# Weight words of the paired heads moved from 128 to 64 bytes into their buffers

## The chip, the cores and the metric

The kernel runs on one core of one Trainium2 chip. The metric is the device time of one launch in microseconds (us), the lowest being best. Before the change it took 828.53 us (median of 3 runs, 827.48 to 829.98).

## The reference

One decoder block on x (1 x 512 x 2048, float32). A normed input is multiplied by w_in (2048 x 6808) to give queries, keys, values and gate paths of two head groups. Group A has 8 heads of 128 with compressed, selected and windowed attention; group B has 16 heads of 64 with a window of 128 and a sink. Both are gated, joined, multiplied by w_out (2048 x 2048), added to x and normed again.

```
h = _rmsnorm(x, norm_g[l]);  proj = h @ w_in[l]
(qa, kca, vca, ksa, vsa, kwa, vwa, za, ga, qb, kb, vb, zb) = jnp.split(proj, offsets, axis=-1)
o_a = gates[..., 0:1] * o_cmp + gates[..., 1:2] * o_sel + gates[..., 2:3] * o_win
y_a = o_a.reshape(B, S, WIDTH_A) * jax.nn.silu(za)
o_b = _banded_attention(qb, _rope(kb), vb, WIN_B, sink=sinks);  y_b = o_b * jax.nn.silu(zb)
x = x + jnp.concatenate([y_a, y_b], axis=-1) @ w_out[l];  return _rmsnorm(x, final_g)
```

## The kernel before

All products of float32 data are made of two words per number, a high word (`hi`, rounded by the copy into float32r) and the rest (`lo`). `mm3` (L126) gives one product as three matmuls: high by high, low by high, high by low. ScalarE makes the high word of a unit of 1,024 weights per partition and VectorE the low one (`split`, L642 to L644, for the paired heads; `load_unit`, L89 to L99, elsewhere).

**Where the words lie.** `words(place)` (L86) takes a buffer of 1,088 float32 words per partition, which is 4,352 bytes or 17 times 256, and hands out 1,024 of them that begin `place` words in. There are three such buffers for the high and three for the low words, and they turn over. Three places are in use: MOVING = 0, EVEN = 16 (64 bytes) and STILL = 32 (128 bytes). In the built program every one of the six buffers begins 128 bytes past a multiple of 256. So words at MOVING lie 128 bytes past a multiple of 256, words at EVEN 192 bytes past, and words at STILL 0 bytes past. Every slice of 128 or 256 of them that a matmul takes begins a multiple of 512 bytes further on, so it lies at the same place modulo 256.

**The stages.** (1) To about 206 us: the keys and values of group A, the compressed keys, and head 0. Here either 512 columns of x (`xh`, `xl`) move past weights that stand still, at place EVEN, or the weights move (256 or 408 columns, place MOVING). (2) From 206.85 to 621.23 us: the paired heads, 1 to 14 (`pair`, L689). Here a head's query and gate projection is made by seven half-size products (`prod`, L668) in place of eight: 7 products of 8 steps of 3 matmuls, 168 for a head and 2,352 for the 14, each with 128 weight columns standing still and 256 columns moving. The weights come from `unit` (L658), the only user of STILL. What moves is `xh`, `xl`, `pu` or parts of `VH`, `VL`, `KH`, `KL`; all of these slices begin 192 bytes past a multiple of 256. (3) Head 15 by `plain` (L772), 512 columns moving, place EVEN. (4) From about 685 us: w_out, where the weights move (256 columns, or 512 in its first quarter) and the activations stand still; place MOVING, and EVEN in the first quarter.

In what follows the **step** of a matmul is the place modulo 256 of the weights that are loaded while it runs (those of the next matmul), less the place modulo 256 of its own moving data. It is 64 bytes in stage 2 now (0 less 192, modulo 256), 64 in the attention's own matmuls and in most of stage 4 (192 less 128), and 0 in the 512-column matmuls at place EVEN. Where a paired head's matmul is followed by one of the attention whose still operand (`VH`, `VB` and the like) lies at 192, the step is 0 for one matmul.

**What sets the order.** A scheduler puts the instructions of the attention of the head before between the matmuls of `pair`, from its own model of their times, and `hooks` (L674) do so by hand in heads 8 to 14. So a stretch of the paired heads' matmuls is broken every so often by a few transposes and attention matmuls.

Of the kernel before, what the change touches and what calls it, by code (L numbers as in the profile page):

```python
# [25 lines left out]
SCALE_A = 128 ** -0.5  # L26
SCALE_B = 64 ** -0.5
CMP = 32
MOVING, EVEN, STILL = 0, 16, 32
WARM = 40  # L30
FIRST = 1
TAB_W = 512 + NQ * CMP + 256
# [3 lines left out]
def hybrid_block(ctx, tc, xT, xtm, w0, w1s, w2s, wz, wq, wkb, wo0, wos, cw1, cw2, cpos, rope, tabs, sinks, gT, fg, out):  # L36
# [49 lines left out]
    def words(place):  # L86
        return [wp.tile([P, 1088], F32R, name=nm, tag=nm)[:, place:place + 1024] for nm in ("whi", "wlo")]

    def load_unit(src, width, rawp=None, opening=False, place=EVEN):  # L89
        rw = rawp.tile([P, 1024], F32, name="raw", tag="raw") if rawp else raw()  # L90
        hi, lo = words(place)
        last["dma"] = (nc.scalar if opening else nc.sync).dma_start(rw[:, :width], src).ins
        if opening:
            dve.tensor_copy(hi[:, :width], rw[:, :width])
        else:
            last["hi"] = act.activation(hi[:, :width], rw[:, :width], AF.Copy).ins  # L96
        last["lo"] = dve.tensor_tensor(out=lo[:, :width], in0=rw[:, :width], in1=hi[:, :width].bitcast(F32),  # L97
                                       op=ALU.subtract).ins
        return hi, lo  # L99
# [81 lines left out]
    for k in range(KT):  # L181
        if k == 0:
            hi, lo = load_unit(w0[0, :, 0, 0:512], 512, opening=True)
            xr = load_x(k)
        else:
            xr = load_x(k)
            hi, lo = load_unit(w0[0, :, k // 2, (k % 2) * 512:(k % 2) * 512 + 512], 512)
# [150 lines left out]
    for u in range(KT // 2):  # L338
        hi, lo = load_unit(w0[1, :, u], 1024)
# [302 lines left out]
    def split(hi, lo, src):  # L642
        act.activation(hi, src, AF.Copy)  # L643
        last["lo"] = dve.tensor_tensor(out=lo, in0=src, in1=hi.bitcast(F32), op=ALU.subtract).ins  # L644
# [11 lines left out]
                nc.sync.dma_start(k[1][:, CMP:].bitcast(F32).rearrange("p (m c) -> p m c", c=256), fw[0, e])  # L656

    def unit(raw):  # L658
        hi, lo = words(STILL)
        split(hi, lo, raw)  # L660
        return hi, lo

# [26 lines left out]
    def pair(h, early=(), hooks=None):  # L689
# [26 lines left out]
        if wide:  # L716
            d = wb.tile([P, 256], F32, name="dd", tag="dd")
        x1 = load(c1, 3)
        u0 = unit(x1)
        x2 = load(c2, 0)  # L720
        u3 = unit(x2)
        if wide:
            sm = load(c5, 0, 2)
# [10 lines left out]
        prod(pa[:, H0], u3, "p", True, hooks)  # L734
        plus(d, d, pa[:, H0])
        u2 = unit(x3)
        prod(pb[:, H0], u2, "21", False, hooks)
        act.activation(zr[:, H1], pb[:, H0], AF.Copy)
# [365 lines left out]
    for u in range(8):  # L1104
        hi, lo = load_unit(wo0[:, u], 1024)
# [354 lines left out]
```

## Time and profile before

| | |
|---|---|
| median of 3 runs | 828.53 us (827.48 to 829.98) |
| the profiled execution | 826.69 us, its span from first to last instruction 824.9 us |
| TensorE matmuls | busy 797.2 us, 97% of the span |
| weight loads | busy 750.0 us, 91% |
| VectorE, ScalarE | 83%, 64% |
| mean granted clock of TensorE | 0.999 of full speed |

The span is the core's time from first to last instruction; the rest of the execution's time lies around it. A matmul's row has its start and how long it took. Matmuls overlap, so the time that one costs is the distance from its start to the start of the next, while its own duration also holds its way through the array. Starts are given to 10 ns, so a distance is read over many matmuls, or from durations, which are given in ns.

### The profile page before, as it was taken

The numbers are of one execution on the slowest core, as the hardware profiler recorded it, in microseconds if no ns is written. First come the engines' busy times: TensorE is split into PE (matmuls) and PEld (weight loads), VectorE is DVE, ScalarE is ACT, GpSimd is POOL, SyncE is SP. The second block draws the span as 40 slices with busy tenths as digits, with TensorE's granted clock in tenths as the row PEclk, the third lists the DMA queues.
The fourth block names the chain that finished last, engine by engine and source line by source line (L and its number), as shares of the span: only waits on it lengthen the run. The fifth ranks groups of instructions, "written<-read, shape, count | busy, mean of one in ns | idle before, by whom it ended". The sixth has DMA issues, their size and how long they took to land.

```text
span 824.9 us, 15435 instructions
## 1 busy us (share of the span) xinstructions
PE 797.2 (97%) x5782; PEld 750.0 (91%) x5782; DVE 685.4 (83%) x1271; ACT 529.4 (64%) x1103; POOL 76.4 (9%) x69
## 2 busy tenths in 40 slices
PE   9999999999999999999999989999999999999996
PEld 8788898988999999999999989989888788999996
DVE  7869786865898989998898789989977588977895
ACT  6734456662677867868776568766866776553545
POOL 4500002012011011011010000000000000000000
PEclk9999999999999999999999999999999999999999
DMA  9655886899712314412321685656595336597835
GB/s 320 206 200 166 290 301 195 272 333 353 223 52 66 104 40 141 154 51 79 116 78 63 195 206 135 186 145 166 139 314 183 91 102 218 138 302 181 259 79 204
DMA packets 60954, 145.29 MB, mean 176 GB/s; under 512 B 6352, under 2 KB 19920, under 8 KB 60880
## 3 DMA queue, kind: packets, MB, share of 16 engines
q1 hardware_dynamic: 57424, 132.26, 48.7%
q0 software_dynamic: 3168, 11.54, 8.1%
q8 instruction: 45, 0.74, 0.4%
q10 hardware_dynamic: 288, 0.52, 0.2%
q14 instruction: 29, 0.24, 0.1%
HBM read 121.65 MB, written 20.55 MB: 172 GB/s over the span
## 4 chain that ended last, share of the span: by engine, by line
PE 75%; DVE 9%; ACT 6%; DMA 5%; issue 3%; POOL 1%; SPq 0%; DVEq 0%; ACTq 0%
PE pj L127 13%; PE pj L129 13%; PE pj L128 13%; PE oa L128 4%; PE oa L129 4%; PE oa L127 4%; PE bank L129 4%; PE bank L127 4%; PE bank L128 3%; PE sp L567 3%; DVE wlo L644 2%; DMA raw<-wq 2%; ACT whi L643 1%; DVE raw L703 1%; DMA xr<-xT 1%
## 5 line engine op out<-in xcount | busy, mean ns | idle before, releaser
L127 PE MATMUL pj<-xh,whi 128*128 128x256 f32 (+1 forms) x560 | 170.7, 305 | 8.7 <-DVE sums L907 2.6
L129 PE MATMUL pj<-xh,wlo 128*128 128x256 f32 (+1 forms) x560 | 170.1, 304 | 1.7 <-DVE wlo L644 1.7
L128 PE MATMUL pj<-xl,whi 128*128 128x256 f32 (+1 forms) x560 | 168.8, 301 | 0.0
L643 ACT ACTIVATE whi<-raw 128x1024 fp32r<-128x1024 f32 x98 | 103.0, 1054 | 55.3 <-PE pj L128 33.2
L644 DVE TENSOR_TENSOR wlo<-raw,whi 128x1024 fp32r<-128x1024 f32 x98 | 121.4, 1242 | 12.7 <-ACT whi L643 12.3
L127 PEld LDWEIGHTS pj<-xh,whi 128*128 128x128 f32 x560 | 105.4, 188 | 15.8 <-ACT whi L643 3.0
L129 PEld LDWEIGHTS pj<-xh,wlo 128*128 128x128 f32 x560 | 105.6, 189 | 7.0 <-DVE wlo L644 2.5
L128 PEld LDWEIGHTS pj<-xl,whi 128*128 128x128 f32 x560 | 105.4, 188 | 4.2
L97 DVE TENSOR_TENSOR wlo<-raw,whi 128x512 fp32r<-128x512 f32 (+2 forms) x74 | 81.3, 1104 | 33.5 <-ACT whi L96 33.0
L96 ACT ACTIVATE whi<-raw 128x1024 fp32r<-128x1024 f32 (+1 forms) x73 | 65.5, 901 | 53.1 <-PE pj L128 17.3
L127 PE MATMUL pj<-pu,whi 128*128 128x256 f32 x224 | 64.2, 287 | 2.9 <-DVE sums L908 1.5
L129 PE MATMUL pj<-pu,wlo 128*128 128x256 f32 x224 | 63.2, 282 | 0.5 <-DVE wlo L644 0.5
L128 PE MATMUL pj<-pu,whi 128*128 128x256 f32 x224 | 63.3, 283 | 0.0
L703 DVE TENSOR_TENSOR raw<-raw 128x1024 f32<-128x1024 f32 x46 | 59.1, 1285 | 0.2
L128 PE MATMUL oa<-wlo,xh 128*128 128x256 f32 (+1 forms) x168 | 50.9, 303 | 0.7 <-DVE wlo L1008 0.7
L127 PE MATMUL oa<-whi,xh 128*128 128x256 f32 (+1 forms) x168 | 50.4, 303 | 1.0 <-DVE sums L904 1.0
L129 PE MATMUL oa<-whi,xl 128*128 128x256 f32 (+1 forms) x168 | 50.3, 302 | 0.0
L127 PEld LDWEIGHTS pj<-pu,whi 128*128 128x128 f32 x224 | 42.3, 189 | 4.2 <-issue 1.6
L129 PEld LDWEIGHTS pj<-pu,wlo 128*128 128x128 f32 x224 | 42.3, 189 | 1.0 <-DVE wlo L644 0.9
L128 PEld LDWEIGHTS pj<-pu,whi 128*128 128x128 f32 x224 | 42.2, 188 | 0.0
L536 DVE TENSOR_TENSOR pl<-tp,ph 128x512 fp32r<-128x512 f32 x56 | 37.7, 683 | 4.9 <-ACT ph L535 4.8
L535 ACT ACTIVATE ph<-tp 128x512 fp32r<-128x512 f32 x56 | 32.1, 588 | 12.4 <-PE tp L930 8.4
(372 smaller groups left out, 2325.6 us busy)
## 6 DMA issues: line engine op xcount, KB each, us to landing
raw<-wq SPq DMA_DIRECT2D x65, 512.0 KB, 4.1
raw<-cw SPq DMA_DIRECT2D x16, 512.0 KB, 5.2
raw<-wos SPq DMA_DIRECT2D x15, 512.0 KB, 5.0
raw<-wq POOLq DMA_DIRECT2D x10, 512.0 KB, 5.5
rw<-wos SPq DMA_DIRECT2D x10, 512.0 KB, 5.2
xr<-xT SPq DMA_DIRECT2D x16, 256.0 KB, 5.1
raw<-w SPq DMA_DIRECT2D x8, 512.0 KB, 4.4
fd<-ft SPq DMA_DIRECT2D x4, 1024.0 KB, 6.0
```

Source lines behind the costliest of these rows:

```text
L96: last["hi"] = act.activation(hi[:, :width], rw[:, :width], AF.Copy).ins
L97: last["lo"] = dve.tensor_tensor(out=lo[:, :width], in0=rw[:, :width], in1=hi[:, :width].bitcast(F32), op=ALU.subtract).ins
L127: pe.matmul(ps, ah, bh, start=first, stop=False, skip_group_check=go_on)
L128: pe.matmul(ps, ah, bl, start=False, stop=False, skip_group_check=go_on)
L129: recent["mm"] = pe.matmul(ps, al, bh, start=False, stop=last, skip_group_check=go_on).ins
L535: act.activation(ph, tp, AF.Copy)
L536: dve.tensor_tensor(out=pl, in0=tp, in1=ph.bitcast(F32), op=ALU.subtract)
L567: pe.matmul(sp[:, a:b], qq[:, qs], kk[0][:, ko:ko + b - a], start=pi == 0, stop=pi == 2)
L643: act.activation(hi, src, AF.Copy)
L644: last["lo"] = dve.tensor_tensor(out=lo, in0=src, in1=hi.bitcast(F32), op=ALU.subtract).ins
L703: return dve.tensor_tensor(out=out, in0=a, in1=b, op=op).ins
```

## The change

`unit` takes its words from place EVEN, 64 bytes into the buffer, in place of STILL, 128 bytes in, and the name STILL goes. The weights of the paired heads then begin 192 bytes past a multiple of 256, as the data that move past them do, and the step of their matmuls is 0 in place of 64. Nothing else differs: in the built programs the same instructions stand in the same order on every engine, and the buffers lie where they lay.

```
-MOVING, EVEN, STILL = 0, 16, 32
+MOVING, EVEN = 0, 16
...
     def unit(raw):
-        hi, lo = words(STILL)
+        hi, lo = words(EVEN)
         split(hi, lo, raw)
         return hi, lo
```

## Rows read from the trace of the kernel before

**Rows 1.** The page: engines' busy time, and the granted clock in 40 slices.
```profile
PE 797.2 (97%) x5782; PEld 750.0 (91%) x5782; DVE 685.4 (83%) x1271; ACT 529.4 (64%) x1103; POOL 76.4 (9%) x69
...
PEclk9999999999999999999999999999999999999999
```

**Rows 2.** Chain of waits, 205 to 620 us: share of the stretch by line.
```profile
by line: PE pj L127 17.1%; PE pj L129 16.6%; PE pj L128 16.3%; PE sp L567 5.9%; DVE wlo L644 4.3%; issue 4.1%; DMA raw<-wq 3.1%; ACT whi L643 2.9%; DVE raw L703 2.6%; PE tp L605 2.3%; PE op L611 1.4%; PE op L613 1.4%; PE op L612 1.4%; DVE t
```

**Rows 3.** Waits, 205 to 620 us: us in total, times, longest.
```profile
ACT whi L643 <- PE pj L128: 27.0, 16, 4.2
```

**Rows 4.** Timeline, TensorE, 206 to 621 us: first and last matmul of the paired heads.
```profile
206.85 0.28 PE L127 MATMUL pj<-xh,whi 128*128 128x256 f32 x1
...
621.23 0.28 PE L129 MATMUL pj<-KH,wlo 128*128 128x256 f32 x1
```

**Rows 5.** Timeline near 355 us: a matmul and the weight load beside it, then 357 us.
```profile
355.28 0.28 PE L128 MATMUL pj<-xl,whi 128*128 128x256 f32 x1
355.28 0.19 PEld L129 LDWEIGHTS pj<-xh,wlo 128*128 128x128 f32 x1
...
357.43 0.28 PE L129 MATMUL pj<-xh,wlo 128*128 128x256 f32 x1
```

**Rows 6.** Timeline near 400 us: first and last of ten paired-head matmuls.
```profile
400.11 0.28 PE L129 MATMUL pj<-xh,wlo 128*128 128x256 f32 x1
...
401.17 0.28 PE L129 MATMUL pj<-xh,wlo 128*128 128x256 f32 x1
```

**Rows 7.** Groups by form, 355.29 to 357.4 us: count, busy us, mean ns.
```profile
L128 PE MATMUL pj<-xl,whi 128*128 128x256 f32 x7 | 1.9, 276 | 0.0
```

**Rows 8.** Groups by form, 400.12 to 401.1 us.
```profile
L129 PE MATMUL pj<-xh,wlo 128*128 128x256 f32 x3 | 0.8, 281 | 0.0
```

**Rows 9.** Groups by form, 230.8 to 231.14 us: around one step of 0.
```profile
L611 PE MATMUL op<-ph,VH 128*128 128x256 f32 x1 | 0.3, 288 | 0.0
L128 PE MATMUL pj<-xl,whi 128*128 128x256 f32 x1 | 0.3, 283 | 0.0
...
L127 PE MATMUL pj<-xh,whi 128*128 128x256 f32 x1 | 0.3, 281 | 0.0
```

**Rows 10.** Timeline, 357.5 to 358.1 us: behind a step of 0 at 357.43.
```profile
357.55 0.28 PE L611 MATMUL op<-ph,VH 128*128 128x256 f32 x1
...
358.02 0.28 PE L127 MATMUL pj<-pu,whi 128*128 128x256 f32 x1
```

**Rows 11.** Timeline, 42 to 46 us: 512 columns, step 0, first and last of ten.
```profile
42.83 0.39 PE L127 MATMUL bank<-xh,whi 128*128 128x512 f32 x1
...
44.87 0.39 PE L127 MATMUL bank<-xh,whi 128*128 128x512 f32 x1
```

**Rows 12.** Timeline, 628 to 631 us: 512 columns, step 0, behind attention matmuls.
```profile
628.45 0.40 PE L128 MATMUL pj<-xl,whi 128*128 128x512 f32 x1
628.68 0.40 PE L129 MATMUL pj<-xh,wlo 128*128 128x512 f32 x1
628.91 0.39 PE L127 MATMUL pj<-xh,whi 128*128 128x512 f32 x1
629.14 0.40 PE L128 MATMUL pj<-xl,whi 128*128 128x512 f32 x1
629.38 0.39 PE L129 MATMUL pj<-xh,wlo 128*128 128x512 f32 x1
629.61 0.39 PE L127 MATMUL pj<-xh,whi 128*128 128x512 f32 x1
...
630.51 0.39 PE L128 MATMUL pj<-xl,whi 128*128 128x512 f32 x1
```

**Rows 13.** Groups by form: the units' words on VectorE and ScalarE.
```profile
L644 DVE TENSOR_TENSOR wlo<-raw,whi 128x1024 fp32r<-128x1024 f32 x98 | 121.4, 1242 | 12.7 <-ACT whi L643 12.3
L97 DVE TENSOR_TENSOR wlo<-raw,whi 128x1024 fp32r<-128x1024 f32 x42 | 51.6, 1229 | 28.1 <-ACT whi L96 27.8
L643 ACT ACTIVATE whi<-raw 128x1024 fp32r<-128x1024 f32 x98 | 103.0, 1054 | 55.3 <-PE pj L128 33.2 <-DVE raw L703 12.8 <-issue 3.2
L96 ACT ACTIVATE whi<-raw 128x1024 fp32r<-128x1024 f32 x42 | 44.4, 1058 | 45.5 <-PE pj L128 17.3 <-PE bank L129 9.1 <-DMA raw<-cw 5.8
```

## The prediction

> **What bounds the kernel now.** I read the page first. TensorE is busy 97% of the span and its clock was granted in full in every slice, that is at 2.4 GHz [rows 1]; so it is the engine to look at, and no clock step is mixed into its times. Then the chain of waits over the stretch of the paired heads: the three matmul lines of `pair` hold 17.1 + 16.6 + 16.3 = 50.0% of 415 us, 207.5 us of it [rows 2]. The waits say the same from the other side: ScalarE stands 27.0 us, 16 times, until a paired-head matmul has let go of a buffer of words [rows 3]. So most of what one of these matmuls costs more or less reaches the end of the program.
>
> Next, what one of them costs. The stretch runs from the first to the last of the rows [rows 4] and holds 2,352 of these matmuls. Two rates stand there for the same shape at the same place. From 355.28 to 357.43 us there are 19 intervals in 2.15 us, 113.2 ns each [rows 5]; from 400.11 to 401.17 us nine intervals in 1.06 us, 117.8 ns each [rows 6]. In the first a matmul's own duration is 276 ns, in the second 281 [rows 7, 8]. I call the first the free rate (113.3 ns, half of what [rows 11] below give for twice the columns) and the second the stalled one; they lie 4.5 ns apart. Both have step 64, and 256 columns at 2.4 GHz would take 106.7. No engine is waited for in either. The load of the next weights starts within 10 ns of the matmul beside which it runs [rows 5], so two reads run side by side for the whole of it, and how they fall against each other is what can differ.
>
> I took the starts of all matmuls between the two rows of [rows 4] from the timeline and kept intervals of 112 to 126 ns between two paired-head matmuls: 2,106 intervals in 145 unbroken runs. Together they are 5.6 us above 113.3 ns each. All stalled would be 2,106 x 4.5 = 9.5 us, so a little under 60% of them are stalled today. Once a run is free it stays so, and once stalled it mostly stays stalled; what turns one into the other is a break: a wait, or attention matmuls between.
>
> **The change part by part.** It changes 2,352 weight loads' addresses, and the output address of 98 writes of high and 98 of low words. No instruction, wait or DMA moves.
>
> *The words' writes.* ScalarE takes 1,054 ns for a unit at place 128 bytes and 1,058 at the other places; VectorE 1,242 and 1,229 [rows 13]. So 98 of them would be +0.4 us and -1.3 us. ScalarE's lies in its waits for TensorE [rows 3]; `wlo` holds 4.3% of the stretch, 18 us of the chain [rows 2], against 98 x 1.24 = 122 us of work, so 15% of -1.3 us is -0.2 us. I take nothing.
>
> *The matmuls.* What I need is the rate of 256 columns with step 0 in a row, and the trace has no such row. The nearest ones are three.
> (a) 512 columns with step 0. In a steady stretch 9 intervals take 2.04 us, 226.7 each [rows 11], which is twice 113.3: free. But behind attention matmuls it takes time to get there: from 628.45 to 629.61 us five intervals take 1.16 us, 26 ns more than five free ones; from then on, 629.61 to 630.51, four take 0.90, free again [rows 12].
> (b) Single steps of 0 at 256 columns, where a paired head's matmul runs beside a load of `VH` or `VB`. Entered from the stalled rate, such a matmul lasts 283 ns where its neighbour has 281, and the next 288 [rows 9]: a step of 0 makes it worse. Of 35 such places, 23 had intervals of 120 ns or more, 122 as a rule at most.
> (c) Entered from the free rate the step itself costs nothing in 52 of 62 places, but the free rate is gone behind it: the matmul at 357.43 us is the last free one [rows 5], and the four intervals from 357.55 to 358.02 take 0.47 us, 117.5 each [rows 10]. Of the 50 places where another 256-column matmul followed such a free step of 0, none stayed free: 45 had 117 to 119 ns, the others more.
> So at this width every step of 0 that I can see either costs more or is followed by the stalled rate. The 512-column rows have 226.7 ns for one weight load, the 256-column ones 113.3; a load that is held up a little has room to catch up in the first and hardly any in the second. By that I expect that the paired heads lose their free runs: 117.8 ns throughout, and the first interval of each run at some 120.7 as in the crossings. Sum: 1,961 x 4.5 = 8.8 us and 145 x 7.4 = 1.1 us, 9.9 us above free, against 5.6 now: +4.3 us of TensorE time.
>
> *What of it reaches the end.* 2,352 matmuls at 116.0 ns (113.3 + 5.6 us / 2,106) are 273 us; 207.5 us of these stand in the chain [rows 2], 76%. So +4.3 us gives +3.3 us. The rest goes into waits of TensorE for VectorE, ScalarE and DMA that get shorter by as much. The profiled execution took 826.7 us, which gives 830.0; it lies 1.8 us under the median of the runs, so by the median I say 831.8 us.
>
> *Bounds.* From below: all 2,106 free, -5.6 us of TensorE time, -4.3 us, 824.2. From above: every interval at 122 ns, the top of what the single steps show, 2,106 x (122 - 116.0) = 12.6 us, x 0.76 = +9.6, 838.1. The value taken lies between, at the stalled rate, since that is what follows a step of 0 in [rows 10].
>
> **The rivals.** *First, it settles as the 512 columns do (not slower).* The first 107 ns of a 512-column matmul with step 0 look the same as a 256-column one with it: the same two addresses, the same start of the load. Those rows end free every time [rows 11, 12], and the single steps in (c) cost nothing themselves. Then every run pays its entry and is free behind it. With the extra ns of [rows 12] in order (about 5, 9, 1, 6 and 4, cut off where a run is shorter), 145 runs pay 3.5 us in place of 5.6: -2.1 us, x 0.76 = -1.6, 826.9 us. With entries as cheap as one stalled interval (5 ns, 0.7 us in all) it is -4.9 x 0.76 = -3.7, 824.8. It decides where runs are longer than about six matmuls; they are 14.5 on the mean. Against it: (b) and (c).
>
> *Second, the place does nothing.* Both rates stand at one and the same step today [rows 5, 6], so something other than the place picks between them, and a break does it. Then the mix stays: 0, and 828.5 us. The Trainium skill says so outright: "Loading the next tile's weights doesn't steal SBUF read bandwidth from the running matmul" (TensorE: Matmul & The Clock Gate, Step-by-step: what each phase is for), and its SBUF page (SBUF — State Buffer, Who interferes with whom) gives TensorE two independent read ports. By that rule there would be one rate and no place to tune. The trace agrees only in part: rows of 113.2 and 117.8 ns for one shape with no wait in either are two rates, though they do not show that the place makes them.
>
> *Third, worse than stalled.* Inside a run each matmul goes on paying what (b) shows, 120 to 122 ns; this is the far end of the forecast's own direction: +6.4 to +9.6 us, 835 to 838. I count it with the forecast.
>
> **How the numbers follow.** Stalled throughout or worse 48% (a quarter of that worse), settled 27%, no effect 25%. A difference under 0.3%, 2.5 us, can't be told from none. The forecast is slower by over that in 0.40 and within it in 0.08; the settled case is faster by over that in 0.15 (cheap entries) and within it in 0.12; no effect gives 0.18 within it and 0.04 and 0.03 beside it. So faster 0.19, same 0.38, slower 0.43. The range for 8 in 10 goes from 825 (most of the settled case) to 836 (stalled, with half of the worse end). The forecast's own range is 830 to 836.
>
> **What would show it.** The paired heads' matmuls at step 0: long stretches with durations of 281 ns and intervals of 118 (forecast); 276 and 113.3 a few matmuls behind each break (first rival); both as now, about 60 to 40 (second); 283 and over throughout (third). The 512-column stretches and the w_out stage must keep their intervals. The chain's share of the three `pj` lines should rise a little, and ScalarE's waits for TensorE grow, if it is slower. The forecast is wrong if a free run of twenty or more paired-head matmuls stands anywhere behind a break; the sum is wrong if the 76% does not hold, which the waits of TensorE in that stretch would tell (they would have to change by more than a quarter of the gain or loss).

## The result, and the profile after

The changed kernel is slower: 832.95 us (median of 11 runs, 830.28 to 835.36) against 828.53 (11 runs, 824.32 to 830.01), a ratio of 1.0065 with a 95% interval of 1.0048 to 1.0082, which is 5.4 us (4.0 to 6.8); the two medians by themselves lie 4.4 us apart. The forecast was 831.8, with a range of 825 to 836. (One execution of a later run, e5, took 4,483.65 us and is left out.)

The profiled execution took 835.06 us, 8.4 more than the one before. The page first, as in [rows 1]: the span, the engines' busy time and the granted clock.

```profile
span 833.3 us, 15435 instructions
PE 804.0 (96%) x5782; PEld 757.1 (91%) x5782; DVE 685.6 (82%) x1271; ACT 530.0 (64%) x1103; POOL 77.6 (9%) x69
PEclk9999999999999999999999999999999999999999
```

TensorE is busy 6.8 us longer with the same 5,782 matmuls at the same clock, and its weight loads 7.1 us longer. VectorE and ScalarE do what they did. So the matmuls themselves have become longer, and the page says no more than that. Where, the first and last rows of the paired heads and the first row behind them tell. They answer to [rows 4], of which the last row is the last paired matmul. Columns: start in us, length in us.

```profile
209.42 0.28 PE L127 MATMUL pj<-xh,whi 128*128 128x256 f32 x1
...
629.77 0.28 PE L129 MATMUL pj<-KH,wlo 128*128 128x256 f32 x1
629.89 0.40 PE L127 MATMUL pj<-xh,whi 128*128 128x512 f32 x1
```

| us | before | after | difference |
|---|---|---|---|
| start to the first paired-head matmul | 206.85 | 209.42 | +2.6 |
| first to last paired-head matmul | 414.4 | 420.4 | +6.0 |
| from there to the end of the span | 203.7 | 203.5 | -0.2 |

The first line has no matmul of the change in it. The kernel before, run once more (e7 below), needed 208.3 us there, and the other runs' traces have 207.2 to 209.1, so this part differs between executions by itself. The +6.0 belong to the paired heads. Now the stretch that [rows 5] showed free and [rows 10] showed behind a step of 0. It is the same place in the program; the timeline of TensorE:

```profile
360.42 0.28 PE L127 MATMUL pj<-xh,whi 128*128 128x256 f32 x1
...
361.02 0.28 PE L129 MATMUL pj<-xh,wlo 128*128 128x256 f32 x1
...
362.10 0.28 PE L129 MATMUL pj<-xh,wlo 128*128 128x256 f32 x1
362.22 0.29 PE L611 MATMUL op<-ph,VH 128*128 128x256 f32 x1
```

From 360.42 to 362.10 there are 14 intervals in 1.68 us, 120.0 each, where 113.2 stood. The durations tell the same (groups by form, 361 to 363 us: count, busy us, mean ns): 282 and 283 ns, where [rows 7] has 276.

```profile
L127 PE MATMUL pj<-xh,whi 128*128 128x256 f32 x5 | 1.4, 283 | 0.0
L128 PE MATMUL pj<-xl,whi 128*128 128x256 f32 x5 | 1.4, 282 | 0.0
```

Counted as in the forecast, 2,109 intervals in 144 runs are 12.8 us above 113.3 ns each, 6.07 a piece, so an interval costs 119.4 ns in the mean. Before it was 5.6 us. Only 31 are free, each of them alone, 497 lie between 117 and 119, 1,527 at 120 or above. The first interval behind a break costs 118.1 in the mean, the eleventh 120.1.

Two more views, both of 207 to 624 us: the chain by line (answers to [rows 2]), and ScalarE's wait for a buffer of words (answers to [rows 3]).

```profile
by line: PE pj L127 18.9%; PE pj L129 18.4%; PE pj L128 18.0%; PE sp L567 5.3%; DVE wlo L644 4.3%; issue 3.7%; PE tp L605 2.4%; DVE tt L573 1.5%; DVE ttb L904 1.5%; PE op L611 1.5%; PE tp L930 1.5%; DVE raw L703 1.5%; PE op L612 1.5%; PE op
```

```profile
ACT whi L643 <- PE pj L128: 31.7, 17, 4.3
```

The three lines hold 55.3% of 417 us now, 230.6, against 207.5. That is 23 us more in the chain for some 7 us more of work: other work that used to end last now ends earlier than a matmul does. So a chain's share says which engine holds the end, and it moves with the change itself. ScalarE waits 4.7 us longer for TensorE.

What the forecast wanted unchanged is so. The words' writes at place EVEN answer to [rows 13] (1,242 and 1,054 ns there), and w_out's matmuls, 660 to 800 us, still last 281 ns (the last line stands in the trace of before in the same words):

```profile
L644 DVE TENSOR_TENSOR wlo<-raw,whi 128x1024 fp32r<-128x1024 f32 x98 | 121.3, 1241 | 13.1 <-ACT whi L643 12.6
L643 ACT ACTIVATE whi<-raw 128x1024 fp32r<-128x1024 f32 x98 | 103.1, 1055 | 56.3 <-PE pj L128 35.1 <-DVE raw L703 11.6 <-issue 2.8
```

```profile
L129 PE MATMUL oa<-whi,xl 128*128 128x256 f32 x128 | 35.9, 281 | 0.0
```

One thing that the change does not touch did change: the first stage's 256-column matmuls, in the mean 115.0 ns from start to start before, have 117.1 now, 0.6 us in all. Run e7 comes back to it.

### The profile page after: what moved, and what is told of

It is laid out like the page before. It is cut to its first block, busy times and chain, and to the rows that moved or that the text cites. A ratio compares the mean times of both kernels' runs of the same rounds, so it can differ in the third digit from the quotient of the medians.

```text
span 833.3 us, 15435 instructions
## 1 busy us (share of the span) xinstructions
PE 804.0 (96%) x5782; PEld 757.1 (91%) x5782; DVE 685.6 (82%) x1271; ACT 530.0 (64%) x1103; POOL 77.6 (9%) x69
## 4 chain that ended last, share of the span: by engine, by line
PE 78%; DVE 10%; DMA 4%; ACT 4%; issue 3%; POOL 0%; SPq 0%; DVEq 0%; ACTq 0%; POOLq 0%
PE pj L127 14%; PE pj L129 14%; PE pj L128 14%; PE oa L128 4%; PE oa L129 4%; PE oa L127 4%; PE bank L129 4%; PE bank L127 4%; PE bank L128 3%; PE sp L567 3%; DVE wlo L644 2%; PE tp L930 1%; PE tp L605 1%; DMA raw<-w 1%; DMA raw<-cw 1%
## 5 line engine op out<-in xcount | busy, mean ns | idle before, releaser
L643 ACT ACTIVATE whi<-raw 128x1024 fp32r<-128x1024 f32 x98 | 103.1, 1055 | 56.3 <-PE pj L128 35.1
```

## The experiments

The theory: the distance between the two places, the step, sets what a 256-column matmul costs beside a load. The rivals: it is where the weights lie by themselves, or it is the work of the other engines and the place does nothing.

### m1_places and m2_entries: the matmuls by themselves

Both compute none of the block. They run a chain of matmuls on TensorE with nothing else on the chip's core beside it, and each line of code holds one pair of places. m1 runs 30 matmuls a line, once behind a wait and once behind four transposes. m2 runs 20 a line with four entries: a wait, four transposes, one transpose, one matmul of step 0. The change in a line is the place alone:

```
+for j in range(30): pe.matmul(ps[:, 0:256], w(48, j), x(48, j, 256), ...)   # weights 192, moving 192: step 0
+turn()                                                                     # four transposes
+for j in range(30): pe.matmul(ps[:, 0:256], w(48, j), x(48, j, 256), ...)   # again
+clear(256)                                                                 # ScalarE copies the bank: a wait
+...                                                                        # the next pair of places
```

> This kernel computes none of the block: it only runs runs of 30 float32r matmuls (128 still columns, a new weight slice each) with nothing else busy, one source line for each pair of places: step 0 to 240 bytes in steps of 16 with the moving data at 192, steps 0, 64, 128 and 192 with the moving data at 0, 64 and 128, and 512 columns at four steps; each pair once behind a wait and once behind four transposes. Theory A (the step between the two reads makes the rate): at 256 columns, step 0 at 118 to 120 ns a matmul, step 64 at 113.3 or 118, the same for all four places of the moving data; at 512 columns step 0 at 226.7, step 192 at 229 to 230. Rival B (the weights' own place makes it: slices that begin at 0 modulo 256 are the good ones): step 64 with moving data at 0, 64 or 128 is slow, and every pair with the weights at 0 is fast, whatever the step. Rival C (other engines' accesses make the stalls, or the place does nothing): one rate, 113.3 ns, on every line.

The timeline of m1 puts a line's 30 matmuls in one row: start, then length from the first's start to the last's end. L74 moves at 192 with step 64, L90 step 128, L106 step 192; L122 moves at 0 with step 0, L126 with step 64.

```profile
53.75 3.70 PE L74 MATMUL ps<-X,W 128*128 128x256 f32 x30
85.43 3.72 PE L90 MATMUL ps<-X,W 128*128 128x256 f32 x30
117.21 3.70 PE L106 MATMUL ps<-X,W 128*128 128x256 f32 x30
148.60 3.76 PE L122 MATMUL ps<-X,W 128*128 128x256 f32 x30
156.41 3.56 PE L126 MATMUL ps<-X,W 128*128 128x256 f32 x30
```

Take off the last one's own duration and divide by 29: L122 gives (3.76 - 0.283) / 29 = 119.9 ns, L126 (3.56 - 0.276) / 29 = 113.2. The durations are in the groups by form:

```profile
L122 PE MATMUL ps<-X,W 128*128 128x256 f32 x30 | 3.8, 283 | 0.0
...
L126 PE MATMUL ps<-X,W 128*128 128x256 f32 x30 | 3.6, 276 | 0.0
```

Steady rates in ns, from the starts of each line:

| moving at | step 0 | 64 | 128 | 192 |
|---|---|---|---|---|
| 192 | 120.0 | 117.7 | 118.7 | 117.8 |
| 0, 64 or 128 | 120.0 | 113.3 | 118.7 | 117.8 |

At moving 192, further steps, behind transposes, gave 118.4 (16), 118.3 (32), 117.7 (48), 118.9 (80), 117.4 (96), 119.8 (112), 120.0 (144), 120.1 (160), 118.2 (176), 116.7 (208), 116.8 (224), 117.2 (240). For steps 0, 128 and 192 the rate is the same wherever the pair lies, and for one place of the weights it is not: the theory stands, and both rivals fall. Step 0 stands at the dear end, with 112, 144 and 160. Step 64 is the only one of these that was free, though not always: at moving 192 it stood at the stalled rate.

> This kernel computes none of the block either. It maps steps 48 to 80 and 192 to 252 in steps of 4 bytes, moving data at 192, and step 64 for the other places, 20 matmuls each behind a wait, behind four transposes, behind one transpose and behind one matmul of step 0. Theory A: near step 64 both 113.3 and about 118 ns, by what stands ahead; the free rate is lost behind a single matmul of step 0, as in the traces of the kernel; at the other steps one rate each whatever stands ahead. Rival: what stands ahead does not matter, the same rate in all four runs of a step.

What turns step 64 from free to stalled, in m2's groups by form: L89 to L95 are step 64 at moving 192, behind a wait, four transposes, one transpose, one matmul of step 0. L119 is step 76 behind one matmul of step 0.

```profile
L89 PE MATMUL ps<-X,W 128*128 128x256 f32 x20 | 2.6, 283 | 0.1
L91 PE MATMUL ps<-X,W 128*128 128x256 f32 x20 | 2.4, 276 | 0.0
L93 PE MATMUL ps<-X,W 128*128 128x256 f32 x20 | 2.4, 276 | 0.0
L95 PE MATMUL ps<-X,W 128*128 128x256 f32 x20 | 2.5, 281 | 0.0
...
L119 PE MATMUL ps<-X,W 128*128 128x256 f32 x20 | 2.4, 276 | 0.0
```

(The first matmul behind a wait lasts longer and lifts L89's mean; its steady rate is 113.3 ns.) One matmul of step 0 is enough to lose the free rate, and all 20 behind it stay stalled: this is (c) of the forecast by itself. But it isn't the only thing that does. At moving 0, step 64 was stalled behind all four entries here, though free in m1; at moving 128 it was lost behind one transpose (the first interval there is 201 ns, as it is behind a wait, so it may have been more than the transpose). So step 64 has two rates, and which one comes depends on what ran before in a way that these runs don't resolve. Steps 52 and 76 were at 113.3 behind all four entries.

One part of what was expected missed: that every other step has one rate. Step 240, start and length behind four transposes and behind one matmul of step 0:

```profile
239.14 2.56 PE L227 MATMUL ps<-X,W 128*128 128x256 f32 x20
...
244.06 2.51 PE L231 MATMUL ps<-X,W 128*128 128x256 f32 x20
```

With the last one's 280 ns taken off, divided by 19, these are 120.0 and 117.4 ns, and m1 had 117.2. Step 200 had 120.0 behind transposes and 117.3 behind the matmul of step 0, 244 120.2 and 118.5; 236 and 204 went the other way, 117.7 to 119.8 and 120.1 to 122.4. So 64 is not alone in having two rates, a matmul of step 0 does not always make those behind it dearer, and step 0's 120.0 is not the top.

### e1, e2, e3: other steps in the kernel

The kernel before with one number changed, so that the paired heads have step 128, 192 or 224:

```
-MOVING, EVEN, STILL = 0, 16, 32
+MOVING, EVEN, STILL = 0, 16, 48    # e1_step128; 0 in e2_step192, 8 in e3_step224
```

> The paired heads' words begin 192 bytes into their buffers, so their step is 128. Theory A (the step sets the rate, as mapped without any other engine at 118.7 ns for step 128, 120 for step 0, 113.3 or 117.8 for step 64): 118.7 ns through the runs, 2,106 x 2.7 = 5.7 us more TensorE time than before, some 0.7 of it at the end: +4.0 us, ratio 1.005. Rival B (only step 0, the same place modulo 256, is bad, and any other step is as good as 64): ratio 1.000.

> The paired heads' words begin at the start of their buffers, step 192. Theory A: 117.75 ns as mapped, never the free rate: 2,106 x 1.75 = 3.7 us of TensorE time, +2.6 us, ratio 1.003. Rival B: 1.000.

> The words begin 32 bytes into their buffers, step 224. Theory A: 116.7 ns as mapped, close to the mean of 116.0 that the kernel before has from its mix: +1.5 us of TensorE time, +1.0 us, ratio 1.001. Rival B: 1.000. If the rates mapped without other engines do not carry over to the kernel, the order of these three and of step 0 will not be the map's.

| | ratio (95%) | mean interval, ns | above free, us | free of some 2,100 | first paired-head matmul to the first row behind the last, us |
|---|---|---|---|---|---|
| before (step 64) | 1 | 116.0 | 5.6 | 871 | 414.5 |
| change (step 0) | 1.0065 (1.0048 to 1.0082) | 119.4 | 12.8 | 31 | 420.5 |
| e1 (step 128) | 1.0041 (1.0017 to 1.0065) | 118.6 | 11.2 | 68 | 420.5 |
| e2 (step 192) | 1.0019 (0.9996 to 1.0042) | 117.1 | 7.8 | 358 | 417.1 |
| e3 (step 224) | 1.0018 (0.9997 to 1.0039) | 117.0 | 7.6 | 342 | 416.6 |

The order is m1's (120.0, 118.7, 117.8, 116.8), though the last two lie nearer to each other here, and the ratios follow the TensorE time. e2 and e3 by themselves can't be told from no change; their intervals in the trace can. The free intervals of the change, e1 and e3 stand among dearer ones, as they do in m1 at step 224; e2's do not. It was expected never to be free, and it has free runs of up to 38 intervals, 113.3 each, beside others of 117.8: step 192 too has two rates here, where m1 and m2 had one.

### e4_lo_only: one step of 0 in three

High words at STILL as before, only the low words moved to EVEN. Of the three matmuls of a product, only the one that runs while low words are loaded has step 0:

```
-        hi, lo = words(STILL)
+        hi, lo = [wp.tile([P, 1088], F32R, name=nm, tag=nm)[:, o:o + 1024]
+                  for nm, o in (("whi", STILL), ("wlo", EVEN))]
```

> Half of the change: high words stay at place 128 bytes, low words go to 64. Of the three matmuls of a step only the one that runs beside the load of the low words has step 0, the other two have 64. Theory A1 (one step of 0 is enough to lose the free rate, as behind single steps in the traces): no free runs at all, (117.8 + 117.8 + 120) / 3 = 118.5 ns, 2,106 x 2.5 = 5.3 us of TensorE time, some 0.7 of it at the end, +3.7 us, ratio 1.0045. Rival A2 (each matmul pays for its own step alone, and the two others keep their mix): a third of what the whole change cost, +1.5 us to +1.8, ratio 1.002.

1.0040 (1.0023 to 1.0056); 9.3 us above free, 62 free, 1,817 of 2,082 intervals at 117 to 119. One of its runs, first and last row:

```profile
504.85 0.28 PE L127 MATMUL pj<-xh,whi 128*128 128x256 f32 x1
...
510.03 0.28 PE L129 MATMUL pj<-xh,wlo 128*128 128x256 f32 x1
```

44 intervals in 5.18 us, 117.7 each. If a matmul of step 0 were dear by itself (120.0) and the two others free (113.3), this would be 115.5. So one such matmul in three takes the free rate from its neighbours as well, and the rate that it leaves is the stalled one; three in three leave 120.

### e5, e6 and e9: the steps that m2 found free

```
-MOVING, EVEN, STILL = 0, 16, 32
+MOVING, EVEN, STILL = 0, 16, 35    # e5_step76; 0, 16, 29 in e9_step52; 3, 16, 35 in e6_step76_52 (w_out's step 52)
```

> The paired heads' words begin 140 bytes into their buffers, step 76, which the map of entries gives 113.3 ns whatever stands ahead. Theory A: nearly all intervals free, entries from other steps a few ns: 5.6 us of TensorE time gone less some 1 us for entries, 0.7 of it at the end: -3 us, ratio 0.996. If the free rate of the map needs the quiet of a kernel with nothing else running, the mix stays and the ratio is 1.000; if words that do not begin at a multiple of 16 bytes cost ScalarE and VectorE more, their 98 rows a piece last longer and the gain shrinks.

> As the run with step 76 for the paired heads, and the moving weights begin 12 bytes into their buffers, so that the w_out stage and the compressed keys have step 52 in place of 64, the other step that the map gives 113.3 ns. Theory A: the w_out stage, stalled nearly throughout in the kernel before (1,025 intervals at 118), goes free too: -4.6 us of TensorE time, and there TensorE holds the chain nearly alone: -4 us more, ratio 0.991 to 0.992. If the rate depends on the moving data's own place as well, which the map tried at multiples of 64 alone, the w_out stage stays at 118 and the ratio is that of the other run.

> The paired heads' words begin 116 bytes into their buffers, step 52, the other step that the map gave 113.3 ns behind everything tried. With step 76 the kernel had more free intervals (1,350 of 2,103 against 871) but 483 at 120 and over, so it had a second, slower rate that the map did not show. If step 52 has none, some 90% are free, 4 to 5 us of TensorE time gone, ratio 0.996; if it has one too, ratio 0.999 to 1.001.

All three missed: 0.9993 (0.9974 to 1.0013), 1.0017 (1.0000 to 1.0033) and 1.0000 (0.9982 to 1.0018). e5's trace says why. Two of its stretches, first and last row of each:

```profile
422.26 0.28 PE L129 MATMUL pj<-pu,wlo 128*128 128x256 f32 x1
...
425.50 0.28 PE L129 MATMUL pj<-xh,wlo 128*128 128x256 f32 x1
...
475.56 0.28 PE L127 MATMUL pj<-VH,whi 128*128 128x256 f32 x1
...
478.96 0.28 PE L129 MATMUL pj<-xh,wlo 128*128 128x256 f32 x1
```

27 intervals in 3.24 us are 120.0, 30 in 3.40 are 113.3. Step 76 has two rates as well, and its other one is dearer than that of step 64. e5 has 1,350 free intervals in place of 871 but 483 at 120 or above, together 4.75 us above free, 0.8 us less than before. That is too little to show in the time. e9 has 1,095 free and 485 at 120 or above, 5.8 us. In e6 the paired heads are as in e5 (4.7 us); w_out's 1,001 intervals stayed at 117.8 with not one free. There the moving data lie at 140, which m2 had not tried. Either the distance alone is not the whole rule off the multiples of 64, or this is another rate of step 52; no run tells which.

### e7_before_again: is the mix of free and stalled runs chance?

The kernel before, unchanged, in a second profiled execution.

> The kernel before, a second profile of it. If a break leaves the free or the stalled rate by chance, the share of free intervals in the paired heads differs between executions, and with it the time; if the schedule fixes it, the same runs are free in both.

829.72 us; 851 free intervals, 5.64 us above free, 414.8 us from the first paired-head matmul to the first row behind the last. Put side by side with the first profile, 94% of the intervals between paired-head matmuls (1,970 of 2,106) are of the same kind, free or not; by chance it would be 52%. So in the paired heads it is for the most part the order of the program that sets what a break leaves behind. Its first part took 208.3 us and the part behind the paired heads 205.0, which is how far these differ without any change.

Elsewhere the order does not set it. The first stage has the same matmuls in the same order in the kernels of before and of e5, the change and e1, yet of its 256-column intervals, some 298, there were free: 189 before, 190 in e7, 192 in e5, but 47 in the change and 21 in e1. In e2, w_out, which e2 does not touch, went free behind a wait, at 730 us, and mostly stayed so to the end. Groups by form, 740 to 800 us, before and then e2:

```profile
L129 PE MATMUL oa<-whi,xl 128*128 128x256 f32 x64 | 18.0, 281 | 0.0
...
L129 PE MATMUL oa<-whi,xl 128*128 128x256 f32 x67 | 18.5, 276 | 0.0
```

Behind the paired heads 695 of 1,031 intervals are free in e2, against 24 of 1,039 before, 3.0 us less for TensorE. In both places the rate turns behind a wait. What picks it there stays open, and since one execution of each kernel was traced (of before, two), so does how much of each ratio came from such stretches.

### e8_wout_step0: the same change in another stage

The weights of the paired heads stay; the moving words of w_out (and those of the first stage) go to place 192, so that these 256-column matmuls have step 0:

```
-MOVING, EVEN, STILL = 0, 16, 32
+MOVING, EVEN, STILL = 16, 16, 32
```

> The change made elsewhere: the paired heads keep step 64, and the moving weights (MOVING) begin 64 bytes into their buffers, so the w_out stage and the 256-column work of the first stage get step 0 in place of 64. Theory A: some 1,190 intervals go from 117.8 (nearly all stalled there already) to 120, about 2.5 to 3 us of TensorE time, the paired heads as before; at some 0.8 of it +2 to +2.5 us, ratio 1.0025 to 1.003. Rival E (what the change cost came from the paired heads' mix with attention, the changes between step 0 and 64, and not from step 0 itself): this stage has long unbroken runs, so ratio 1.000.

1.0034 (1.0013 to 1.0054), 2.8 us. The paired heads are as before (876 free, 5.5 us above free). In w_out the mean interval went from 117.70 to 119.66 ns, +2.0 us over 1,001, and the first stage's rose by 1.4 us in all (with its step at 64 as before, it rose by 0.6 in the change and by 0.8 in e1, so not all of this need be the step). The group that stood at 281 ns in the changed kernel:

```profile
L129 PE MATMUL oa<-whi,xl 128*128 128x256 f32 x128 | 36.2, 283 | 0.0
```

The same step costs the same in other code with the roles of weights and activations exchanged. That it would be something of the paired heads alone falls.

## Why the prediction was right

*Direction and mechanism.* Right. No step-0 stretch stays free: 31 free intervals of 2,109, no two in a row, where twenty in a row would have said that the forecast is wrong; and m2 shows one matmul of step 0 taking the free rate from 20 behind it. The reading of single steps in the trace before ((b) and (c)) carried this.

*The rate taken.* Here the sum went wrong in its size, by the term for the intervals behind the first of each run. The forecast took 117.8 ns throughout, since that is what follows one step of 0 in [rows 10]. Those rows have a step of 0 once and then 64 again: they show what 64 is like when it is not free, and not what 0 is like in a row. In a row it is 120.0 (m1, 360.42 to 362.10 us of the change). The entry was off too, and to the other side: 120.7 forecast for the first interval, 118.1 measured, with the rate climbing to 120 over about ten matmuls. In the sum, the first intervals came to 0.7 us in place of 1.1, all others to 12.1 in place of 8.8: 12.8 against 9.9. So +7.2 us of TensorE time, not +4.3. The nearest row for the dear rate was there: 283 ns beside the single step of 0 in [rows 9], which is the duration that step 0 has in m1 at 120.0. The "third rival" had it, as its lower end.

*What reaches the end.* +6.0 us of +7.2 came through in the paired heads of this execution, 83%, against 76% forecast. The ratio's 5.4 us (4.0 to 6.8) gives 75% (56 to 94), so the two can't be told apart. Nor can one execution's stretch carry such a figure: e6's is 1.4 us longer than that of before, with matmuls 0.9 us cheaper. The 76% itself is a little high, since some 6 of the 207.5 us are 512-column matmuls of head 15 (611.80 to 617.51 us); without them it is 74%, which takes 0.1 us from the sum.

*The sum.* By the forecast's share, 7.2 x 0.76 = +5.5 us, inside what the runs show (4.0 to 6.8). Since some stretches turn by themselves (e7), it may be luck that it lies so near the middle. The forecast's +3.3 lies below the measured interval; its 831.8 us differs by 1.2 from the median. The direction was forecast, but not firmly: slower had a chance of 0.43, the same 0.38.

*The first rival* (settles as the 512 columns do) is wrong for 256 columns. m1 shows that 512 could not stand in for 256. At moving 192, steps 0 and 64 with 512 columns, L170 and L174:

```profile
246.03 6.96 PE L170 MATMUL ps<-X,W 128*128 128x512 f32 x30
260.84 7.16 PE L174 MATMUL ps<-X,W 128*128 128x512 f32 x30
```

(6.96 - 0.389) / 29 = 226.6 ns for step 0 (226.7 by the starts) and (7.16 - 0.395) / 29 = 233.3 for 64 (233.5 by the starts); 128 gave 232.2 and 192 gave 229.0. Of these four steps the best of the one width is the worst of the other. So the room that the forecast saw for a held-up load beside 512 columns does not settle it: with all of that room, step 64 costs nearly 7 ns more than step 0.

*The second rival* (the place does nothing) is wrong: m1 has 113.3 to 120.0 ns for one shape by place alone, with VectorE busy 1% of the span. The Trainium skill's sentence that loading the next weights "doesn't steal SBUF read bandwidth from the running matmul" (TensorE: Matmul & The Clock Gate, Step-by-step: what each phase is for), and its two independent read ports for TensorE (SBUF — State Buffer, Who interferes with whom) don't agree with this: by them all 256-column lines of m1 would have one rate.

*The words' writes* were rightly taken as nothing, also at places that are no multiple of 16 bytes (e5: 1,055 and 1,243 ns).

*Open.* Why the distance between the two reads matters inside the chip; and what picks the rate that a break or a wait leaves at the steps that have two, in the order of the program or outside it. The writes' own share was not tried apart from the matmuls.

## What to carry to other kernels

Where 256-column float32r matmuls each have a weight load beside them, the place of the weights against the moving data was worth up to 6% of a matmul here (113.3 to 120.0 ns). Look at the starts and the durations (276, 281, 283 ns here) before and after any change of buffers; a duration alone does not give the rate, since step 228 has 281 ns at 120.0 in m2. Keep weights and moving data off the same place modulo 256, but take no other step for free without a measurement. A rate that is to hold for a long stretch must be read from a long stretch; one such instruction among others shows what its neighbours do. And what is best at one width must be measured again at another.

## What the runs showed of the hardware that was not expected

- One shape at one step can have two steady rates, each over fifteen matmuls and more: 113.3 or 117.8 at steps 64 (m1, m2) and 192 (e2), 113.3 or 120.0 at step 76 (e5), 120.0 or 117.2 at step 240 (m2, m1). In the paired heads the program's order mostly fixes which one comes (94% alike in two executions). Behind a wait it can turn with the code unchanged: w_out had 281 ns before and 276 in e2.
- With the moving data at 192, step 0 is the cheapest of four steps for 512 columns (226.7 ns, against 229.0 to 233.5) and the dearest of the same four for 256 (120.0, against 113.3 or 117.7 at step 64, 117.8 and 118.7).
- Places 12 bytes off the usual ones (steps 52 and 76) can be free as well, and cost neither ScalarE nor VectorE anything when they write there (1,055 and 1,243 ns in e5).
